# Turning normalised rows by a product with a diagonal of their roots in a hybrid trunk kernel on one core

## The chip, the cores and the metric

The kernel runs on one core of a Trainium2 chip. A core has five engines that run side by side: TensorE (PE; its weight loads are shown apart as PEld), VectorE (DVE), ScalarE (ACT), GpSimd (POOL) and SyncE (SP, which here only starts DMA transfers). They share a buffer memory of 128 partitions (SBUF); PE writes its results into eight accumulator banks (PSUM), from which DVE and ACT read them. The metric is the device time of one execution in microseconds. Lower is better.

## The reference

One layer over 2048 rows of 1024 channels, all in fp32. What matters for the change is that the rows are normalised three times and that two of these feed products which contract over the channels:

```python
def rmsnorm(x, g):
    y = xf * lax.rsqrt(jnp.mean(xf * xf, axis=-1, keepdims=True) + EPS) * g
...
xn = rmsnorm(x, norm1_g[l])
z = xn @ w_in[l]
u_pool, zq, zf, zi, zo, zg = jnp.split(z, splits, axis=-1)
gates = jax.nn.sigmoid(zg + b_gate[l]).reshape(B, S, N_BRANCHES, D_MODEL)
ya = pool_mixer(u_pool, pool_w[l], pool_scale[l]) @ w_pa[l]
yb = hgrn2_mixer(zq, zf, zi, zo, lower_bounds[l], hgrn_norm_g[l]) @ w_pb[l]
merged = gates[:, :, 0] * ya + gates[:, :, 1] * yb
x = x + merged @ w_o[l]
x = x + conv_glu_ffn(rmsnorm(x, norm2_g[l]), w_up[l], conv_w[l], conv_b[l], w_down[l])
return rmsnorm(x, final_g)
```

The root of a row is one number for each row; the gain `g` is one number for each channel.

## The kernel before

**Tiling.** The 2048 rows are four row blocks of 512 rows (`TB`), each of four row tiles of 128 rows (`NT`, index j). The 1024 channels are eight column blocks of 128 (index k). Two row blocks at a time go through the mixer (`mixer`, b0 = 0 and 2) and then through the feed-forward part (`ffn`). The large products are done by a Strassen scheme of seven products in place of eight (P1 to P7), each operand split into a high and a low part and multiplied in three products of 128x128 by 128x512, all through the helper `mm` (L157 and L158).

**Rows and channels.** The products need the operand with channels on the partitions, but the sum of squares is taken along a row. So a row tile is normalised with rows on the partitions and then turned in blocks of 128x128 on PE. This is done for the first two row blocks of x (called x0 and x1, at the start of the kernel) and for all four row blocks of the mixer's output (m0 and m1 after the first mixer, m2 and m3 after the second). The row blocks 2 and 3 of x come by another way: `channels_a_task` and `channels_b_task` load them with channels on the partitions already, and nothing is turned there.

**The steps for one row tile** (`norm_rows`, L772 to L784). Its two halves of 128x512 (`halves`, from the dictionary `xt`) are squared and summed on ScalarE by `row_rstd` (L762 to L770), which writes the squares into two tiles `t` that nobody reads; GpSimd makes the root's inverse `r`, one number for each row, in two small steps (L768, L769). VectorE then multiplies each half by `r` into the same two tiles `t` (L782), and these become `xs[j, 0]` and `xs[j, 1]`. Last comes `after(j)`: for m it stores the unscaled rows to DRAM for the later sum (`spill_rows`, L881 to L888), for x0 it turns the blocks that are wanted first.

**Turning** (`transpose`, L868 to L870). One call turns the block of row tile j and column block k into a quarter of an accumulator bank, with PE's transpose and the unit matrix `ident`. Four calls (j = 0 to 3) fill the bank of one column block. ScalarE or VectorE then reads the bank, multiplies by the channel gain and writes the operand or its two parts.

**Who calls it.** `forms_a_task` normalises and turns the first row block of a pair (x0, m0, m2) and makes the forms B11 and B21; `forms_b_task` does so for the second (x1, m1, m3) and makes the Strassen differences (T1 to T4, B22). At the very start (`early`) the column blocks 0 to 3 of x0 are turned row tile by row tile, as soon as each is normalised, and between them stand transposes of the unit matrix that only keep PE busy (`warm`, L747 to L752). Everywhere else the four blocks of a column block are turned together. In `forms_b_task` a condition (`go`) holds the turning back until a given place in the stream of products.

**The order.** Tasks are Python generators that are stepped once in every six products of the main stream, so the turning is issued between products. Each engine runs its instructions in the order in which the build put them, and that order is worked out from estimated times (`schedule_with_timeline_sim=True`, L2132). Working tiles come from a pool of 73 buffers of 128x528 (`slot`); a buffer is free when the last instruction that uses its tile is done.

Of the kernel before, what the change touches and what calls it, by code (L numbers as in the profile page):

```python
# [15 lines left out]
ALU = mybir.AluOpType  # L16
AX = mybir.AxisListType

P = 128
# [70 lines left out]
def tile_trunk(  # L90
# [17 lines left out]
    pe, act, dve, pool, sp = nc.tensor, nc.scalar, nc.vector, nc.gpsimd, nc.sync  # L108
# [10 lines left out]
    def slot(name, cols=TB, dt=F32):  # L119
        return slots.tile([P, cols], dt, tag="s", name=name, padded_shape=[P, 528])  # L120
# [249 lines left out]
    kept, keeping, w_both, halves = {}, [], {}, {}  # L370
# [259 lines left out]
    ident = const.tile([P, P], F32, tag="ident", name="ident")  # L630
# [131 lines left out]
    def row_rstd(halves, junk, name):  # L762
        ss = small.tile([P, 4], F32, tag="ssq", name=name + "ss")
        for hf in range(2):
            act.activation(junk[hf], halves[hf], AF.Square, scale=1.0 / 32.0,
                           accum_out=ss[:, hf : hf + 1])
        r = small.tile([P, 4], F32, tag="rstd", name=name + "r")
        pool.tensor_scalar(r[:, 1:2], ss[:, 1:2], ss[:, 0:1], EPS, ALU.add, ALU.add)  # L768
        last_root[0] = pool.tensor_tensor(r[:, :1], r[:, 1:2], neghalf[:, :1], ALU.pow)  # L769
        return r  # L770

    def norm_rows(src, name, xs, after, lag=1):  # L772
        for j in range(NT):
            while (src, j) not in ready:
                yield 1
            halves = [xt[src, j, c] for c in range(2)]
            t = [slot(f"{name}xs{j}_{hf}") for hf in range(2)]
            r = row_rstd(halves, t, f"{name}{j}")
            if lag:
                yield lag  # L780
            for hf in range(2):
                dve.tensor_scalar(t[hf], halves[hf], r[:, 0:1], None, ALU.mult)  # L782
                xs[j, hf] = t[hf]
            after(j)  # L784

    def load_channels(b, k):
# [80 lines left out]

    def transpose(ps, xs, j, k):  # L868
        c = (k % 4) * P
        return pe.transpose(ps[:, j * P : (j + 1) * P], xs[j, k // 4][:, c : c + P], ident)  # L870

    def transposed(xs, k, name, gain, ps=None):
        if ps is None:
            ps = bank(f"{name}t{k}")
            for j in range(NT):
                transpose(ps, xs, j, k)
        t = slot(f"{name}b{k}")
        act.activation(t, ps, AF.Copy, scale=col(gain + k))
        return t
# [10 lines left out]
    def forms_a_task(src, gain, forms, full, after=lambda j: None, early=False):  # L890
# [4 lines left out]
        def rows(j):  # L895
            after(j)
            for k in range(len(pts)):
                ins = transpose(pts[k], xs, j, k)
            if early:
                warm(WARM[1], ins)  # L900

        if early:
            warm(WARM[0])
        yield from norm_rows(src, name, xs, rows)
        yield 6

# [15 lines left out]
        for k in range(len(pts), KD):  # L922
            key = "B11" if k < 4 else "B21"
            if early:
                ps = bank(f"{name}t{k}")
                for j in range(NT):
                    transpose(ps, xs, j, k)
                scaled(k, key, ps)
                t = slot(f"{name}b{k}")
                dve.tensor_scalar(t, ps, col(gain + k), None, ALU.mult)  # L930
                full[key].append(t)
                yield 1
                continue
            t = transposed(xs, k, name, gain)
            yield 1
            full[key].append(t)
            forms[key].append(split(t, f"{name}f{k}", True))

    def forms_b_task(src, gain, forms, full, after, go, early):
        name = f"{src[0]}{src[1]}_"  # L940
        xs = {}
        while early and not forms["B21"]:
            yield 1
        yield from norm_rows(src, name, xs, after, int(early))
        while not go():
            yield 2
# [371 lines left out]
    class Unit:  # L1318
# [34 lines left out]
        def after(self, p):  # L1353
            bk, t = self.bank, self.t
            if p == "P1":
                act.copy(self.tmp("e1"), bk["X"])  # L1356
            elif p == "P6":
                first(dve.tensor_tensor(self.tmp("u2"), t["e1"], bk["Z"], ALU.subtract))
            elif p == "P2":
                self.emit(0, 0, None, bk["X"])  # L1360
            elif p == "P7":
                if self.own:
                    ins = dve.tensor_tensor(self.tmp("u3"), bk["W"], t["u2"], ALU.subtract)
                else:
                    ins = dve.tensor_tensor(self.tmp("u3"), bk["Z"], t["e1"], ALU.subtract)
                first(ins)
                self.forms.setdefault("u3", []).append(ins)
                self.emit(1, 1, (t["u3"], "add"), bk["V"])
            elif p == "P4":
                if self.own:  # L1370
                    self.emit(1, 0, (t["u3"], "add"), bk["Y"])
                else:
                    self.emit(1, 0, (t["e1"], "from"), bk["Z"])
            elif p == "P3":
                self.emit(0, 1, (t["u2"], "sub"), bk["V"])
# [760 lines left out]
```

## Time and profile before

| what | value |
|---|---|
| median of 3 runs | 2460.93 us (2460.14 to 2461.15) |
| the profiled execution | 2461.48 us |
| its span | 2459.8 us |
| instructions in the span | 37972 |
| mean clock granted to PE | 0.999 |
| HBM read / written | 403.55 MB / 200.81 MB |

The page of the profile gives busy times by engine, the chain of work that ended last and the costliest groups of instructions. More precise answers come from views of the same trace: one line's instructions, busy time by stage, the waits of one engine, and the chain in order of time. In the chain a row is a start and a length in us and what the chain went through there; "x4" is the number of instructions merged. In the view of one line, three durations (shortest, median, longest, in ns) stand behind the count. In the view by stage a row is a stretch of time and its length, then the busy time and number of instructions on PE, PEld, DVE, ACT and POOL, then the granted clock, the DMA share and GB/s. In the view of waits a row is who waited for whom, the total in us, how many times, and the longest. Matmuls are pipelined, so the duration of one is longer than the time that it adds to a busy PE.

### The profile page before, as it was taken

The numbers are of one execution on the slowest core, as the hardware profiler recorded it, in microseconds if no ns is written. First come the engines' busy times: TensorE is split into PE (matmuls) and PEld (weight loads), VectorE is DVE, ScalarE is ACT, GpSimd is POOL, SyncE is SP. The second block draws the span as 40 slices with busy tenths as digits, with TensorE's granted clock in tenths as the row PEclk, the third lists the DMA queues.
The fourth block names the chain that finished last, engine by engine and source line by source line (L and its number), as shares of the span: only waits on it lengthen the run. The fifth ranks groups of instructions, "written<-read, shape, count | busy, mean of one in ns | idle before, by whom it ended". The sixth has DMA issues, their size and how long they took to land.

```text
span 2459.8 us, 37972 instructions
## 1 busy us (share of the span) xinstructions
PE 2439.1 (99%) x12624; PEld 1979.3 (80%) x12624; DVE 1903.0 (77%) x3294; ACT 1232.0 (50%) x2372; POOL 750.7 (31%) x1068
## 2 busy tenths in 40 slices
PE   9999999999999999999999999999999999999998
PEld 7887777788888888888888888888888888888887
DVE  7777776997998778876586667768889987878755
ACT  6545544435555445555544555542465554445534
POOL 4343353403354334451210101112033332335310
PEclk9999999999999999999999999999999999999999
DMA  8989888977888779899784443478333444447852
GB/s 283 312 218 277 237 220 238 329 221 245 206 251 242 225 226 240 269 364 321 237 285 153 136 127 122 154 237 306 112 129 129 150 156 134 145 144 260 306 165 99
DMA packets 272612, 529.29 MB, mean 215 GB/s; under 512 B 28640, under 2 KB 49248, under 8 KB 272096
## 3 DMA queue, kind: packets, MB, share of 16 engines
q1 hardware_dynamic: 204560, 348.47, 42.4%
q0 software_dynamic: 42880, 113.27, 18.1%
q10 hardware_dynamic: 24976, 65.13, 7.6%
q8 instruction: 99, 1.62, 0.3%
q14 instruction: 97, 0.79, 0.1%
HBM read 403.55 MB, written 200.81 MB: 246 GB/s over the span
## 4 chain that ended last, share of the span: by engine, by line
PE 92%; DVE 3%; DMA 2%; ACT 1%; issue 1%; POOL 0%; SPq 0%; ACTq 0%; DVEq 0%; POOLq 0%
PE dn_P L158 17%; PE up_Z L158 15%; PE up_X L158 10%; PE up_V L158 10%; PE wo_P L158 6%; PE gr_V L158 3%; PE pb L158 3%; PE gr_X L158 3%; PE io_Z L158 2%; PE io_V L158 2%; PE gr_W L158 2%; PE gr_Y L158 2%; PE fr_X L158 1%; PE gr_Z L158 1%; PE fr_V L158 1%; PE ur_X L158 1%
## 5 line engine op out<-in xcount | busy, mean ns | idle before, releaser
L260 ACT CAST ops<-raw 128x512 fp32r<-128x512 f32 x802 | 493.4, 620 | 784.8 <-PE dn_P L158 161.5
L266 DVE TENSOR_TENSOR ops<-raw,ops 128x512 fp32r<-128x512 f32 x774 | 571.4, 743 | 240.9 <-ACT ops L260 232.6
L1872 DVE SCALAR_TENSOR_TENSOR e<-h,cols,e 128x512 f32<-128x512 f32 x176 | 142.9, 817 | 30.3 <-ACT e L1870 26.9
L1870 ACT ACTIVATE e<-h,cols 128x512 f32<-128x512 f32 x176 | 142.2, 814 | 25.3 <-DVE h L1316 18.9
L1875 DVE SCALAR_TENSOR_TENSOR e<-h,cols,e 128x512 f32<-128x512 f32 x176 | 133.9, 770 | 2.5
L1125 POOL DMA_DIRECT2D g_P<-dg_P x154 | 83.0, 541 | 171.8 <-PE dn_P L158 133.0
L1441 POOL TENSOR_TENSOR gf_P<-e,e 128x512 f32<-128x512 f32 x44 | 61.1, 1390 | 149.5 <-DVE e L1881 85.8
L1441 POOL TENSOR_TENSOR gf_P<-gf_P,e 128x512 f32<-128x512 f32 x44 | 58.2, 1322 | 74.1 <-DVE e L1881 71.6
L501 POOL TENSOR_TENSOR raw<-raw,raw 128x512 f32<-128x512 f32 x32 | 46.5, 1453 | 90.7 <-DVE ops L266 81.8
L1879 ACT ACTIVATE e<-e 128x512 f32<-128x512 f32 x88 | 55.6, 632 | 36.6 <-DVE e L1875 36.4
L1865 POOL COPY h<-h 128x2 f32<-128x2 f32 x88 | 39.3, 459 | 106.6 <-DVE h L1315 103.8
L1316 DVE TENSOR_TENSOR h<-up_u,up_V 128x512 f32<-128x512 f32 x88 | 60.1, 683 | 10.5 <-PE up_V L158 10.0
L1867 POOL COPY hist<-h 128x2 f32<-128x2 f32 x88 | 35.2, 400 | 101.5 <-DVE h L1316 99.3
L1413 DVE TENSOR_TENSOR x<-x,wo_P 128x512 f32<-128x512 f32 x88 | 55.8, 678 | 11.8 <-PE wo_P L158 11.7
L1865 POOL COPY h<-hist 128x2 f32<-128x2 f32 x88 | 45.0, 517 | 55.4 <-DVE h L1316 25.1
L1581 POOL TENSOR_TENSOR q<-q,qs 128x512 f32<-128x512 f32 x16 | 22.3, 1393 | 119.2 <-ACT qs L1580 119.2
L1413 DVE TENSOR_TENSOR ac<-ac,dn_P 128x512 f32<-128x512 f32 x72 | 47.3, 681 | 11.5 <-PE dn_P L158 11.0
L1614 ACT ACTIVATE gt<-gt,cols 128x512 f32<-128x512 f32 x48 | 34.8, 724 | 42.5 <-DVE gt L1316 41.3
L1356 ACT COPY up_e<-up_X 128x512 f32<-128x512 f32 x44 | 25.8, 587 | 60.1 <-PE up_X L158 38.6
L1895 POOL DMA_DIRECT2D dg_P<-gf_P x88 | 50.7, 576 | 8.9 <-POOL gf_P L1441 7.2
L758 POOL TENSOR_SCALAR ro<-so 128x4 f32<-128x4 f32 x16 | 4.1, 256 | 151.3 <-ACT sq L1289 151.1
L1755 POOL TENSOR_TENSOR ya<-ya,gl 128x512 f32<-128x512 f32 x24 | 35.8, 1512 | 47.2 <-DVE ya L1752 39.6
(1335 smaller groups left out, 7855.2 us busy)
## 6 DMA issues: line engine op xcount, KB each, us to landing
g_P<-dg_P POOLq DMA_DIRECT2D x154, 256.0 KB, 5.9
raw<-in_w_up_t SPq DMA_DIRECT2D x132, 256.0 KB, 3.1
raw<-in_w_in_t SPq DMA_DIRECT2D x98, 256.0 KB, 3.7
dg_P<-gf_P POOLq DMA_DIRECT2D x88, 256.0 KB, 3.8
dg_P<-e SPq DMA_DIRECT2D x66, 256.0 KB, 3.2
raw<-in_w_dn SPq DMA_DIRECT2D x66, 256.0 KB, 5.4
x<-in_x SPq DMA_DIRECT2D x64, 256.0 KB, 5.2
gd<-gt ACTq DMA_DIRECT2D x64, 256.0 KB, 3.6
```

Source lines behind the costliest of these rows:

```text
L158: count[1] = pe.matmul(*args, **kw)
L260: self.mark = act.copy(hi, v)
L266: low = self.low = dve.tensor_tensor(lo, v, f32(hi), ALU.subtract)
L1125: eng.dma_start(t, d)
L1316: return dve.tensor_tensor(dst, t, ps, ALU.add if how == "add" else ALU.subtract)
L1413: dve.tensor_tensor(t, t, ps[j], ALU.add if sg > 0 else ALU.subtract)
L1441: pin(eng.tensor_tensor(t, x0, x1, op))
L1865: pool.tensor_copy(h[:, 0:2], hist[:, mt] if hf == 0 else hs[s, 0][:, TB : TB + 2])
L1870: in_turn(act.activation(t, h[:, 2:], AF.Identity, bias=col(o_cb + mt), scale=col(o_cw + 4 * MF + mt)))
L1872: in_turn(second(dve.scalar_tensor_tensor(t, h[:, 1 : 1 + TB], col(o_cw + 2 * MF + mt), t, ALU.mult, ALU.add)))
L1875: dve.scalar_tensor_tensor(t, h[:, 0:TB], col(o_cw + mt), t, ALU.mult, ALU.add)
L1879: in_turn(act.activation(g, g, AF.Silu))
```

## The change

VectorE no longer scales the rows. For each row tile it multiplies the 128x128 unit matrix by the row tile's inverse root, which gives a diagonal matrix; the four diagonals of a row block stand side by side in one new working tile (`roots`). The blocks of the unscaled halves are turned by an ordinary fp32 product with that diagonal instead of a transpose with the unit matrix. The product of a block's transpose with the diagonal scales each row by its root, so that the bank holds what it held before. The tiles `t` now hold only the squares.

```diff
@@ -774,13 +774,16 @@
             while (src, j) not in ready:
                 yield 1
             halves = [xt[src, j, c] for c in range(2)]
+            if not j:
+                roots = slot(f"{name}dg")
             t = [slot(f"{name}xs{j}_{hf}") for hf in range(2)]
             r = row_rstd(halves, t, f"{name}{j}")
             if lag:
                 yield lag
             for hf in range(2):
-                dve.tensor_scalar(t[hf], halves[hf], r[:, 0:1], None, ALU.mult)
-                xs[j, hf] = t[hf]
+                xs[j, hf] = halves[hf]
+            xs[j] = roots[:, j * P : (j + 1) * P]
+            dve.tensor_scalar(xs[j], ident, r[:, 0:1], None, ALU.mult)
             after(j)
 
     def load_channels(b, k):
@@ -867,7 +870,8 @@
 
     def transpose(ps, xs, j, k):
         c = (k % 4) * P
-        return pe.transpose(ps[:, j * P : (j + 1) * P], xs[j, k // 4][:, c : c + P], ident)
+        return pe.matmul(ps[:, j * P : (j + 1) * P], xs[j, k // 4][:, c : c + P], xs[j],
+                         start=True, stop=True)
 
     def transposed(xs, k, name, gain, ps=None):
         if ps is None:
```

## The prediction

> **What bounds the kernel now.** I read the head of the page first, then its chain of work that ended last.
>
> ```profile
> span 2459.8 us, 37972 instructions
> ...
> PE 2439.1 (99%) x12624; PEld 1979.3 (80%) x12624; DVE 1903.0 (77%) x3294; ACT 1232.0 (50%) x2372; POOL 750.7 (31%) x1068
> ...
> PE 92%; DVE 3%; DMA 2%; ACT 1%; issue 1%; POOL 0%; SPq 0%; ACTq 0%; DVEq 0%; POOLq 0%
> ```
>
> PE is busy for 99% of the span and makes up 92% of the chain; DVE, which the change relieves, is 77% busy and makes up 3%. So the first question is not what DVE saves but what each instruction costs on PE. Busy time over the whole span says little about one place, so the next view is busy time by stage. I cut it where blocks are turned: the head (x0 and x1, up to 60 us), the two stretches in which the m rows are turned (583 to 619 and 1790 to 1826 us), and what lies between.
>
> ```profile
> 0.00:14.00 14.00, 9.16 (x61) 8.07 (x61) 5.64 (x16) 8.72 (x22) 6.33 (x19) 1.00 0.87 303
> 14.00:60.00 46.00, 45.00 (x219) 36.82 (x219) 39.05 (x63) 28.73 (x58) 24.03 (x64) 1.00 0.84 275
> 60.00:300.00 240.00, 238.82 (x1745) 192.28 (x1744) 180.73 (x422) 127.46 (x289) 88.67 (x84) 1.00 0.89 262
> 300.00:583.00 283.00, 277.36 (x1469) 223.67 (x1468) 231.01 (x406) 122.23 (x260) 91.09 (x84) 1.00 0.82 251
> 583.00:619.00 36.00, 36.00 (x191) 29.75 (x190) 28.00 (x44) 22.52 (x46) 16.53 (x20) 1.00 0.76 225
> 619.00:1790.00 1171.00, 1170.35 (x6062) 952.07 (x6061) 900.59 (x1558) 584.88 (x1121) 313.95 (x462) 1.00 0.71 222
> 1790.00:1826.00 36.00, 36.00 (x191) 29.80 (x190) 27.98 (x44) 22.74 (x47) 14.21 (x19) 1.00 0.41 136
> ```
>
> The first number after the stage's length is PE's busy time. Both stretches in which m is turned have PE at 36.00 of 36.00 us, so nothing there waits for the scaling that is removed, and any time added to PE there lengthens the run. In the head PE is idle for 14.00 - 9.16 = 4.84 us before 14 us and for 46.00 - 45.00 = 1.00 us from 14 to 60 us. The granted clock is 1.00 everywhere.
>
> **The change part by part.** First, how many blocks are turned, and by how many records. The answer for the transposes' line (L870), and for two lines of the recurrence that serve as a yardstick (L1252 transposes, L1261 an ordinary fp32 product), has these rows.
>
> ```profile
> L870 PE MATMUL m_t<-ident,m_xs x128: 269/272/274, 583.6 to 1824.9; 128*128 128x128 f32 x128
> L870 PE MATMUL x_t<-ident,x_xs x64: 269/273/329, 7.5 to 41.4; 128*128 128x128 f32 x64
> ```
> ```profile
> L1252 PE MATMUL pk<-ident,k x60: 270/273/273, 154.7 to 1606.8; 128*128 128x128 f32 x60
> ```
> ```profile
> L1261 PE MATMUL pv<-v,kt x120: 270/275/276, 161.2 to 1621.2; 128*128 128x128 f32 x120
> ```
>
> Six row blocks (x0, x1, m0 to m3) of 4 row tiles and 8 column blocks make 192 turned blocks, and there are 128 + 64 = 192 records: a transpose is one record. L1252 and L1261 run over the same loop (nk chunks, 4 heads, 4 row blocks, 15 chunks a head in all: 60 calls), but the product leaves 120 records: an ordinary fp32 product of 128x128 by 128x128 is **two records**. The changed line is a product of just this form: fp32 on both sides, 128x128 by 128x128, start and stop set.
>
> Second, what each takes on a busy PE. The durations above (about 0.27 us) overlap and are not it; the chain in order of time gives what each group adds.
>
> ```profile
> 154.88 0.87 PE pk L1252 x8
> ...
> 161.34 0.89 PE pv L1261 x8
> ...
> 168.84 0.22 PE po L1284 x2
> ```
> ```profile
> 585.58 0.44 PE m_t L870 x4
> ...
> 608.15 0.87 PE m_t L870 x8
> ```
>
> A turned block of m takes 0.44 / 4 = 0.11 us of PE. A product takes 0.89 / 4 = 0.2225 us (eight records are four products), and the po row says the same: 0.22 for one. All of these lie inside the same kind of stream of 128x512 products. So each block turned costs **0.2225 - 0.11 = 0.1125 us more on PE**. I take this price for all 192; the rows of product and transpose scatter by less than 0.005 us, so its bounds are 0.11 and 0.115.
>
> The m rows: 128 blocks x 0.1125 = **14.4 us**, all of it in stages where PE has no idle time. Nothing hides it.
>
> The x rows in the head: 64 blocks. The first 16 (columns 0 to 3 of x0) stand in the start, row tile by row tile, each waiting for its scaling; there only the last row tile counts, because PE idles between them.
>
> ```profile
> 12.31 0.50 DVE x_xs L782
> 12.81 0.04 issue
> 12.85 0.66 PE x_t L870 x4
> 13.51 0.55 PE warm L750 x5
> 14.06 5.74 PE io_X L158 x24
> ```
>
> Today the first scaling of 0.50 us lets the four transposes go. The change puts one 128x128 scaling of the unit matrix there. No row shows that operation; the nearest are these, the same operation on 512 columns and on 4.
>
> ```profile
> L782 DVE TENSOR_SCALAR x_xs<-x,x_0r x4: 479/482/488, 7.0 to 25.2; 128x512 f32<-128x512 f32 x4
> ```
> ```profile
> 5.32 0.17 DVE L2077 TENSOR_SCALAR lbt<-lbt 128x4 f32<-128x4 f32 x1
> ```
>
> Between 0.17 and 0.48 us in proportion to the columns I estimate 0.17 + 0.31 x 124 / 508 = 0.25 us. PE then starts the last group at 12.31 + 0.25 + 0.04 = 12.60 us and not at 12.85, but needs 4 x 0.1125 = 0.45 us more before the warming transposes and io_X: **+0.2 us** at the start (+0.1 with 0.17 us, +0.4 with 0.48 us).
>
> The other 48 blocks (columns 4 to 7 of x0, all of x1) follow up to 42 us (the L870 row above) and cost 48 x 0.1125 = **5.4 us**. Against that stands the 1.00 us of idle time from 14 to 60 us. The waits of PE show what it is.
>
> ```profile
> PE io_Z L158 <- ACT ops L260: 0.5, 1, 0.5
> PE io_V L158 <- ACT ops L260: 0.5, 1, 0.5
> ```
>
> Both are waits for a converted weight, and the chain before them leads back through DVE and a DMA, not through PE:
>
> ```profile
> 29.10 0.79 DVE x_xs L782 x2
> ...
> 31.21 0.67 DVE x_xs L782
> 31.88 0.64 DVE w8s L432
> 32.52 0.65 DVE w9s L432
> ...
> 34.97 5.01 DMA kw1ioP<-w9s
> ```
>
> Here is the one place where DVE's relief matters. The eight scalings of x1 are part of the chain that makes the sums w8s and w9s late. They become four of an estimated 0.25 us, so that chain gets shorter by at most 8 x 0.48 - 4 x 0.25 = 2.8 us, while PE comes later by up to 5.4 us. PE then finds its weights ready: I take the whole **1.0 us** off. Were that cover not there (the chain moves with PE), nothing comes off.
>
> What else moves. On DVE 48 scalings of 0.48 us or more go and 24 of about 0.25 us come, some 17 us of DVE busy time in all; in the m stretches PE is at 36.00 of 36.00, so that is worth nothing there. ScalarE's squares and GpSimd's two steps for the root stay as they are. No DMA is added or moved on any queue, the spill of the m rows included. The added wait, of a turning product for its piece of the diagonal, takes the place of the wait for two scaled tiles and ends earlier by one scaling; behind it on PE stands the whole stream, as before. The x and m tiles stay in use until the last product has read them and the tiles of the squares are free at once: eight buffers held change places with eight, and one more of 73 is held for the diagonal. I cost that at nothing; its cover is that PE waits for no buffer in the stretches at 36.00 of 36.00.
>
> **Sum:** 14.4 + 5.4 + 0.2 - 1.0 = 19.0 us. The profiled execution took 2461.48 us, of which 2459.8 are the span; 2461.48 + 19.0 = 2480.5. The median of the runs shown is 2460.93 us, 0.55 us below the profiled one, so I say **2480 us**, 0.8% slower.
>
> One rule of the Trainium skill gives another sum. By the rows, a product is two records of 0.11 us against one for a transpose. The page "TensorE: Matmul & The Clock Gate", section "Terms", calls the transpose mode four times faster for fp32, and "FP8 and Floating Point Precision", section "TensorE Precision Notes", counts four passes for a true fp32 product. By that rule each block would cost three further transposes; the rows of pv and po disagree with it, as they show twice and not four times.
>
> **The rivals.**
> 1. *Four times the transpose.* If the product with the diagonal runs as four passes of 0.11 us, each block costs 0.33 us more: 192 x 0.33 = 63 us, less 1 us, about 2524 us. For it: nothing here shows a product with a diagonal. Against it: pv has the same shapes and types and takes 0.2225 us. Chance 0.03.
> 2. *The second record is hidden: no change.* PEld is 80% busy and PE may set the two records of a product between the long ones at no further cost, as a block has the same data to load. Then the extra cost is nothing, the start gains 0.25 us and the head 1.0 us: about 2460 us. It decides below (4.9 + 1.2) / 192 = 0.032 us of extra cost for a block, where the result is within 0.2%. Against it: the pv group stands in just such a stream and shows no hiding at all. Chance 0.04.
> 3. *Another order.* The build orders each engine's instructions by estimated times, and other instructions give other estimates. PE's idle time outside the head and the tail is 1.18 + 5.64 + 0.65 = 7.5 us (the stages from 60 to 583 us and from 619 to 1790 us, less their busy time). A new order could bring that much again (2488 us) or give it back (2473 us). The largest waits of PE outside the head are these:
>
> ```profile
> PE pl L1155 <- ACT k L1138: 2.3, 3, 1.2
> ...
> PE pa_V L158 <- DVE ya L1752: 1.3, 3, 0.6
> ```
>
>    For it: they are waits of tenths of a microsecond that any shift moves. Against it: none is for a line that the change touches. Chance 0.15, with 0.10 of it on the slow side.
>
> **How the numbers follow.** The forecast has the remaining 0.78; its own range, from the prices' bounds with 0 to 2 us of absorbed idle time, is 2477 to 2484 us. The range of 8 in 10 takes in the third rival on both sides: **2473 to 2488 us**; the first two, 0.07 together, lie outside. About 0.2% (4.9 us) is what a measurement of this kernel can tell from no change. Forecast, first and third rival are slower by more: 0.95 with a small part of the third left out (0.78 + 0.03 + 0.14). The second gives "same" nearly all its 0.04. Faster is left 0.01: the extra cost would have to vanish and more waits than the two above with it.
>
> **What would show each step.** The line of the turning product should have 384 records, two for each block, and its groups should stand in the chain with 0.89 us for four blocks (1.78 for eight) where the transposes have 0.44 (0.87). The stages in which m is turned should each be about 7.2 us longer for the same products, and still full. DVE should show 24 scalings of 128x128 near 0.25 us in place of 48, and a sum lower by about 17 us. The two waits of io_Z and io_V for converted weights should be gone, and the io_X products should enter the chain near 14.3 us, not at 14.06. If the groups take 0.44 us, the second rival holds; if they take 1.76 us, the first. If the m stages are longer by 7.2 us but the sum is off by more than 3 us, the order elsewhere has changed, and the stages from 60 to 583 us will show it. What would make the prediction wrong is above all a price of the product that depends on what stands around it, since 192 of them carry the sum.

## The result and the profile after

| what | before | after |
|---|---|---|
| median of 6 runs each, us | 2461.04 (2460.14 to 2462.88) | 2479.43 (2478.01 to 2480.09) |
| ratio after / before, 95% interval | | 1.0073 (1.006 to 1.0086) |
| profiled execution, us | 2461.48 | 2480.01 |
| its span, us | 2459.8 | 2478.3 |

The change makes the kernel 18.4 us slower; 2480 us was predicted. The head of the page of after gives the span, the busy times and the shares of the chain:

```profile
span 2478.3 us, 38316 instructions
...
PE 2460.0 (99%) x12816; PEld 2001.9 (81%) x12816; DVE 1890.4 (76%) x3270; ACT 1232.9 (50%) x2372; POOL 740.2 (30%) x1068
...
PE 94%; DMA 2%; DVE 2%; ACT 1%; issue 1%; POOL 0%; SPq 0%; ACTq 0%; POOLq 0%; DVEq 0%
```

VectorE does 12.6 us less (1903.0 - 1890.4) and TensorE 20.9 us more, with 192 records more. The span follows TensorE. The view by stage of after, cut where blocks are turned, has the same columns as before:

```profile
0.00:14.00 14.00, 10.87 (x77) 10.02 (x77) 3.46 (x12) 8.95 (x22) 5.08 (x19) 1.00 0.85 295
14.00:60.00 46.00, 46.00 (x251) 39.45 (x250) 35.83 (x57) 28.00 (x58) 21.46 (x64) 1.00 0.86 277
60.00:300.00 240.00, 239.12 (x1746) 192.41 (x1745) 179.29 (x422) 127.30 (x289) 88.07 (x83) 1.00 0.88 257
300.00:583.00 283.00, 276.78 (x1469) 223.46 (x1468) 227.96 (x400) 121.49 (x260) 91.77 (x84) 1.00 0.82 250
583.00:627.00 44.00, 44.00 (x257) 38.33 (x256) 27.78 (x44) 22.96 (x48) 13.66 (x20) 1.00 0.70 216
627.00:1794.00 1167.00, 1166.32 (x6039) 947.23 (x6038) 893.72 (x1544) 580.95 (x1110) 308.97 (x458) 1.00 0.71 221
1794.00:1842.00 48.00, 48.00 (x276) 41.62 (x275) 31.10 (x49) 27.05 (x57) 14.06 (x23) 1.00 0.39 131
```

Three things are to be seen. The stages in which m is turned (583 to 627 and 1794 to 1842 us) are still full. The 1.00 us of idle time from 14 to 60 us is gone. And from 60 to 1794 us, outside those stages, PE is idle for 0.88 + 6.22 + 0.68 = 7.8 us, where it was 7.5 us: no new wait of any size has come. The instructions of the turning line and of the new scaling in after, with shortest, median and longest duration in ns:

```profile
L873 PE MATMUL m_t<-m_dg,x x256: 270/275/276, 587.4 to 1841.9; 128*128 128x128 f32 x128
L873 PE MATMUL x_t<-x_dg,x x128: 270/275/378, 7.3 to 42.9; 128*128 128x128 f32 x128
```
```profile
L786 DVE TENSOR_SCALAR m_dg<-ident,m_0r x4: 280/282/286, 572.9 to 1816.3; 128x128 f32<-128x128 f32 x4
L786 DVE TENSOR_SCALAR x_dg<-ident,x_0r x2: 285/290/294, 7.0 to 24.6; 128x128 f32<-128x128 f32 x2
```

There are 256 + 128 = 384 records where 192 stood. The chain of after in order of time, where m0 and then m1 are turned:

```profile
587.61 0.89 PE m_t L873 x8
588.50 1.40 PE wo_P L158 x6
...
615.65 1.78 PE m_t L873 x16
617.43 1.39 PE up_X L158 x6
```

Four blocks take 0.89 us and eight take 1.78 us, as the pv rows before, and six products of the main stream follow each group without a gap. How late the same product starts in the two kernels shows where the time comes in. The timeline of PE before, and then that of after, at the first product behind the mixer's weights (fr_X) and the first of the feed-forward part (up_X):

```profile
98.64 0.39 PE L158 MATMUL fr_X<-x_f0h,ops 128*128 128x512 f32 x1
...
598.72 0.39 PE L158 MATMUL up_X<-m_f0h,ops 128*128 128x512 f32 x1
```
```profile
102.46 0.39 PE L158 MATMUL fr_X<-x_f0h,ops 128*128 128x512 f32 x1
...
606.21 0.40 PE L158 MATMUL up_X<-m_f0h,ops 128*128 128x512 f32 x1
```

The head costs 102.46 - 98.64 = 3.8 us. By up_X, behind which m1 is still to be turned, it is 606.21 - 598.72 = 7.5 us. The same subtraction at nine products, for every kernel that ran, is the table on which most of what follows rests. Each number is the start of a product in that kernel's profile less its start in the profile of before, in us; the first row has the starts before. Between wo and up lies the turning of m0 (m2 in the second pair), behind up that of m1 (m3).

```
                       io_X   io_Z   fr_X     wo     up   io_X     wo     up   last
                      first  first  first  first  first  2nd pr 2nd pr 2nd pr product
before, start         13.96  42.22  98.65 517.10 598.72 1243.84 1723.87 1805.49 2452.04
after                 -0.02   4.74   3.81   3.84   7.49  12.00  12.23  15.93  18.51
before, again          0.25   0.25  -0.44   0.77   0.75   0.72   0.73   0.74   0.72
after, again          -0.46   4.30   3.38   1.40   5.05   9.55   9.79  13.48  16.07
scaled, product       -0.07   4.74   3.91   1.80   5.44   9.44   9.26  12.68  14.82
unscaled, transpose   -1.53  -2.27  -2.71  -2.89  -2.91  -2.74  -2.71  -2.68  -4.09
m only                -0.08  -0.07  -0.53  -0.65   2.93   7.43   7.61  11.12  14.16
x only                -0.52   4.28   3.36   1.41   1.49   2.83   2.26   2.27  -0.07
x only, again         -0.15   4.61   3.69   1.66   1.70   3.03   2.41   2.42   0.06
product twice          2.68  18.21  17.40  15.00  25.64  36.09  36.71  47.54  57.02
two halves             2.41  17.91  17.04  14.29  25.02  36.36  36.46  47.38  57.32
one record             4.92   4.65   3.86   4.33   4.30   9.95  10.32  10.37  11.37
```

In the row of after, m0 and m2 cost 7.49 - 3.84 = 3.65 and 15.93 - 12.23 = 3.70 us, where 32 x 0.1125 = 3.6 us were predicted. From up to the next mixer it is 4.51 us and from the second up to the last product 2.58 us: m1 and m3 lie in there, with something added to one and taken from the other, to which the runs below come back.

### The profile page after: what moved, and what is told of

Read it like the earlier page. It is cut to its first block, busy times and chain, and to the rows that moved or that the text cites. A ratio compares the mean times of both kernels' runs of the same rounds, so it can differ in the third digit from the quotient of the medians.

```text
span 2478.3 us, 38316 instructions
## 1 busy us (share of the span) xinstructions
PE 2460.0 (99%) x12816; PEld 2001.9 (81%) x12816; DVE 1890.4 (76%) x3270; ACT 1232.9 (50%) x2372; POOL 740.2 (30%) x1068
## 4 chain that ended last, share of the span: by engine, by line
PE 94%; DMA 2%; DVE 2%; ACT 1%; issue 1%; POOL 0%; SPq 0%; ACTq 0%; POOLq 0%; DVEq 0%
PE dn_P L158 17%; PE up_Z L158 15%; PE up_V L158 10%; PE up_X L158 10%; PE wo_P L158 6%; PE gr_V L158 3%; PE pb L158 3%; PE gr_X L158 3%; PE io_Z L158 3%; PE io_V L158 2%; PE gr_W L158 2%; PE fr_X L158 1%; PE gr_Z L158 1%; PE gr_Y L158 1%; PE fr_V L158 1%; PE m_t L873 1%
```

## The experiments

The expectations name theories by letters. **A** is the prediction's: TensorE pays for a second record in each block, and nothing else counts. **B** is the first rival to it, that the product costs more than that and VectorE's relief pays some of it back. **C** is that part of the cost comes from another order of the work behind the head. **D** is that the second record's price depends on what stands around it, so that part of it is hidden. **E** and **F** came up on the way: a pace of the main stream that belongs to the program, and a wait that differs between executions. A time is a median, a ratio stands with its 95% interval, and the kernel before ran beside each on the same chip.

**1. The product without the relief of VectorE.** The rows are scaled as before and turned by an ordinary product with the unit matrix.

```diff
-        return pe.transpose(ps[:, j * P : (j + 1) * P], xs[j, k // 4][:, c : c + P], ident)
+        return pe.matmul(ps[:, j * P : (j + 1) * P], xs[j, k // 4][:, c : c + P], ident,
+                         start=True, stop=True)
```

> VectorE scales the rows as before, and PE turns them by an fp32 product with the unit matrix: the change's PE part alone. Theory A (the time is 192 blocks at 0.1125 us more on PE, and VectorE's relief is worth next to nothing): 2461.0 + 14.4 (m) + 5.4 (x behind the start) + 0.45 (start) less 1 to 1.5 us of idle time in the head = about 2479.5 us, within 1 us of the changed kernel. Theory B (the product costs more than that, and VectorE's 13 us of saved busy time pay part of it back): 3 us or more above the changed kernel, 2482.5 us or more.

Measured: 2477.29 us beside 2461.66 us, +15.6 us, ratio 1.0063 (1.0051 to 1.0076). The chain of this kernel at m0:

```profile
585.55 0.89 PE m_t L870 x8
586.44 1.40 PE wo_P L158 x6
```

The group has the price of after with VectorE's work as before, and the whole cost is not above that of after (+18.4 us, and +16.2 us when it ran again). B would need it above. So B falls: the record accounts for all of it, and no relief is seen. In the head the row is that of after to within 0.1 us (4.74 and 3.91), though VectorE still scales: TensorE's lateness alone covers the two waits for converted weights.

**2. The relief without the product.** The diagonals are made, but the unscaled rows are turned by the transpose with the unit matrix, so that these rows are not normalised.

```diff
-        return pe.matmul(ps[:, j * P : (j + 1) * P], xs[j, k // 4][:, c : c + P], xs[j],
-                         start=True, stop=True)
+        return pe.transpose(ps[:, j * P : (j + 1) * P], xs[j, k // 4][:, c : c + P], ident)
```

> The diagonals are made as in the change, but the unscaled rows are turned by the transpose with the unit matrix: VectorE's part of the change alone. The normalisation of these rows is left out. Theory A: 2460 to 2461 us, at most 1 us below the kernel before, since only the head has a wait behind the scaling. Theory B: 2458 us or less.

Measured: 2457.75 us beside 2461.66 us, -3.9 us, ratio 0.9987 (0.9978 to 0.9996). That is more than A allows (1 us), and it lies in the range given for B (2458 us or less). The chain of this kernel at the start:

```profile
11.79 0.59 ACT x_f0h L912
12.39 0.04 issue
12.43 5.81 PE io_X L158 x24
```

No transpose waits for a root any more, so io_X starts at 12.43 and not at 13.96 us (-1.5 us). Another 1.2 us goes by fr_X (-2.71 in all), where the two waits for weights stood; the m stages give nothing (-2.89 at wo, -2.68 at the second up); the last 1.4 us goes in the second feed-forward part, where it is the pace of the products (232.48 and 231.70 ns in the table under runs 8 to 10, 1840 x 0.78 ns = 1.4 us). So to be rid of the waits for VectorE's scalings is worth some 2.7 us in the head, and nothing in the stages where m is turned. It pays nothing back in after, as run 1 shows.

**3 and 4. The change for one kind of row alone.** For m only, and for x only; the other kind is scaled and transposed as before.

```diff
+            if not j and src[0] == "m":        # "x" in the other kernel
+                roots = slot(f"{name}dg")
...
+                if src[0] == "m":
+                    xs[j, hf] = halves[hf]
+                    continue
...
+        if j not in xs:
+            return pe.transpose(to, rows, ident)
+        return pe.matmul(to, rows, xs[j], start=True, stop=True)
```

> The change for the m rows alone (128 blocks); x as before. Theory A: 2461.0 + 128 x 0.1125 = 2475.4 us, the m stages each 7.2 us longer. Theory C (part of the 18.4 us comes from another order of the work behind the head): less than 12 us or more than 17 us above the kernel before.

> The change for the x rows alone (64 blocks); m as before. Theory A: 48 x 0.1125 = 5.4 us less the two waits of the head, which cost 1.5 us of the stream, and nothing at the start: 2461.0 + 3.9 = 2465 us. If the idle time of 1.0 us is all that goes: 2465.5 us. Theory C: under 2463 or over 2467 us, and not the rest that m only leaves of 18.4 us.

Measured: m only 2476.36 us, +14.7 us, ratio 1.006 (1.0048 to 1.0073); x only 2461.87 us, +0.2 us, ratio 1.0001 (0.9992 to 1.001), both beside 2461.66 us. The m rows cost what the prediction's term says (14.4 us). The x rows should have cost 4.6 us by the prediction and 3.9 us by the expectation above. In the head they come near it: the table has 4.28 us at io_Z and 3.36 us at fr_X. Then it is lost again: 2.0 us by wo, and 2.3 us between the second up and the last product, hundreds of microseconds behind the last x block. A step that costs 3 us where it stands was worth nothing at the end. The time lies in the range given for C (under 2463 us), and the two parts make 14.9 us and not 18.4, as C has it. A, which holds for m only, misses x only by 3 us: what happens behind the head counts too. Runs 8 to 10 ask what it is.

**5. Twice the cost.** Every turning product of after is issued twice.

```diff
+        for _ in range(2):
+            ins = pe.matmul(ps[:, j * P : (j + 1) * P], xs[j, k // 4][:, c : c + P], xs[j],
+                            start=True, stop=True)
+        return ins
```

> The changed kernel with every turning product issued twice into the same place. Theory A (a product is 0.2225 us of a full PE, nothing of it hidden): 176 blocks behind the start x 0.2225 = 39.2 us, and 2.4 us at the start, where the first groups already follow one another: 2479.4 + 41.6 = 2521 us. Theory D (PE has room between the long products, which the second record only partly fills): 2510 us or less.

Measured: 2518.58 us beside 2460.82 us, ratio 1.0233 (1.0218 to 1.0248), 39.2 us over after, where A gave 41.6. The chain of this kernel at m0:

```profile
598.64 1.78 PE m_t L874 x16
600.42 1.39 PE wo_P L158 x6
```

Four blocks take 1.78 us, twice 0.89 to the hundredth. The price doesn't depend on how much of it stands there, and nothing is hidden: D falls. 192 x 0.2225 = 42.7 us would be the plain sum. By the table, against after, the parts with turning give 13.6 us (fr_X), 7.0 (m0), 7.1 (m2) and 6.9 (m3), each near its due (14.2 with the start's 16 blocks, and 7.1 for each m); the stretch from fr_X to wo, without any turning, gives 2.4 us back, and the stretch with m1 1.2 us less than its due. The latter is the pace of the products there (231.39 ns for 232.07 in the table under runs 8 to 10, 1.2 us over the up products).

**6. The same columns in twice the records.** Each product is cut in two, of 64 columns of the diagonal each.

```diff
+        for h in range(0, P, 64):
+            ins = pe.matmul(ps[:, j * P + h : j * P + h + 64], xs[j, k // 4][:, c : c + P],
+                            xs[j][:, h : h + 64], start=True, stop=True)
+        return ins
```

> The changed kernel with every turning product cut into two of 64 columns of the diagonal each: the same columns go through PE, but each block is loaded as a weight four times instead of twice. If the columns streamed set the 0.11 us of a record: 2479.4 us as the changed kernel, four records of 0.055 us. If the weight load sets it: four records of about 0.1 us or more, 2513 us or more.

Measured: 2520.32 us beside 2460.82 us, ratio 1.0247 (1.023 to 1.0265); the four executions lie between 2518.82 and 2528.75 us. The chain of this kernel at m0, and its turning line:

```profile
597.98 1.73 PE m_t L874 x16
599.71 1.46 PE wo_P L158 x6
```
```profile
L874 PE MATMUL m_t<-m_dg,x x512: 217/275/275, 597.8 to 1880.4; 128*128 128x64 f32 x171
```

Sixteen records of 64 columns take 1.73 us, 0.108 us each, where eight of 128 columns take 0.89 us, 0.111 us each. Half the columns cost the same. What a record of this shape costs is thus not its moving columns. Nor does every record cost this much. In the chain of before, 64 records with a stationary block of 32 columns and 48 moving columns take 0.013 us each:

```profile
203.96 0.82 PE pl L1155 x64
```

What is left is the stationary block of 128x128, which is the same in both kernels. That it sets the price is argued, as no run changed it alone. The Trainium skill, page "TensorE: Matmul & The Clock Gate", section "LDWEIGHTS (loading the stationary operand)", gives a load as the stationary operand's columns divided by 1.2, in ns: 128 / 1.2 = 107 ns by estimate, and this trace agrees with 0.108 us for this shape. For 32 columns it would give 27 ns by estimate, where the pl records, which write to separate quarters of the partitions in turn, add 13 ns each: the agreement is for this shape alone.

**7. One record.** VectorE scales the rows into new tiles of type fp32r, and these are turned by an fp32r product with a unit matrix of that type; the rows lose their last bits.

```diff
+                xs["unit"] = slot(f"{name}un", P, F32R)
+                dve.tensor_scalar(xs["unit"], ident, 1.0, None, ALU.mult)
...
+                xs[j, hf] = slot(f"{name}xr{j}_{hf}", dt=F32R)
+                dve.tensor_scalar(xs[j, hf], halves[hf], r[:, 0:1], None, ALU.mult)
...
+        return pe.matmul(ps[:, j * P : (j + 1) * P], xs[j, k // 4][:, c : c + P], xs["unit"],
+                         start=True, stop=True)
```

> VectorE scales the rows as before, but writes them as fp32r, and PE turns them by an fp32r product with a unit matrix in fp32r; the rows lose their last bits. An fp32r product of the main stream is one record. Theory A (the cost is the second record): 2461 us, within 1.5 us of the kernel before, the groups of four blocks at 0.44 us in the chain. If a product costs more than a transpose whatever its records: above 2466 us.

Measured: 2470.05 us beside 2460.82 us, +9.2 us, ratio 1.0036 (1.0023 to 1.0048). The chain of this kernel at m0, and the longest wait of its PE:

```profile
589.88 0.40 PE m_t L873 x4
590.27 2.83 PE wo_P L158 x12
```
```profile
PE x_t L873 <- DVE x_xr L786: 6.5, 3, 3.2
```

With one record a block takes 0.40 / 4 = 0.10 us, and m0 adds nothing (4.33 at wo, 4.30 at up). So an ordinary product isn't dear in itself: its second record is, which here goes away together with the fp32 type. The time that A gave (2461 us) failed all the same, and lies in the range of the theory against it (above 2466 us), which the row of the group refutes. It failed because the start is 4.9 us later (TensorE waits 6.5 us for scaled tiles there) and the stretch with m1 takes 5.7 us more. In that stretch the view by stage shows PE no longer full (PE busy 56.96 of 60.00 us):

```profile
600.00:660.00 60.00, 56.96 (x252) 45.08 (x251) 48.25 (x73) 34.89 (x67) 22.43 (x29) 0.97 0.82 194
```

Why these tiles come so late wasn't tried; only the price of the record and m0 are clean in this run.

**8 to 10. The same programs again.** Before, after and x only ran once more, unedited, each with a new profile.

> The kernel before once more, with its own profile. Theory E (the program's order fixes the waits of the mixer's last stage and the pitch of the main stream): the same wait of about 0.6 us for gr_V, the same 232.5 ns from product to product in the second feed-forward part and 231.7 in the first, as in the profile shown; ratio 1. Theory F (each execution has its own): the wait moves by 1 us or more or the pitch by 0.5 ns or more.

> The changed kernel once more, on one chip with the two others. 2479.4 us by the first measurement, 18.4 us over the kernel before. Theory E: again 2.2 us of waiting for gr_V and 232.07 ns in both feed-forward parts. Theory F: another wait, another pitch, and a time that still differs from 18.4 us by less than 1.5 us, as the turning itself (18.3 us in the profile) does not change.

> The change for the x rows alone once more: 2461.9 us at first, 0.2 us over the kernel before, where its head is 3.2 us longer. Theory E: again within 0.5 us of 2461.9, with a shorter wait for gr_V (0.2 us) and 231.4 ns in the second feed-forward part. Theory F: the head is again 3 to 4 us longer, and the rest comes out otherwise, so that the time lies up to 3.9 us over the kernel before.

Measured, beside 2461.66 us: before 2461.11 us, ratio 0.9999 (0.9989 to 1.0009); after 2477.87 us, ratio 1.0067 (1.0052 to 1.0082); x only 2461.65 us, ratio 1.0002 (0.9993 to 1.0011). All three agree with their first runs within the intervals. What differs between two profiles of one program is one wait, the first row of PE's waits of after and its row in after, again:

```profile
PE gr_V L158 <- DVE gt L1320: 2.2, 1, 2.2
```
```profile
PE gr_V L158 <- DVE gt L1320: 0.4, 1, 0.4
```

The same wait in before, and then in before, again:

```profile
PE gr_V L158 <- DVE gt L1316: 0.6, 1, 0.6
```
```profile
PE gr_V L158 <- DVE gt L1316: 1.8, 1, 1.8
```

In the table the first row of after goes from 3.81 at fr_X to 3.84 at wo, and the second from 3.38 to 1.40: 2.0 us between the two executions, and the wait's 1.8 us is nearly all of it. The chain of after leads back from this wait to a DMA that loads tiles of the mixer again:

```profile
418.58 5.26 DMA mx<-md
...
430.43 0.61 DVE gr_u L1367
431.04 0.02 issue
431.07 0.70 DVE gt L1320
431.76 0.14 issue
431.90 3.01 PE gr_V L158 x12
```

That is F, and for before and after it holds: the same program waits 1 to 2 us longer in one execution than in another. It doesn't hold everywhere. In x only the wait was 0.2 us both times, and after, again lies 2.2 us below its first cost, where F gave 1.5 us at most. A rival stands beside it, that a late head shortens these waits by itself. Between fr_X and wo, six of the eight profiles with a late head lose 2.0 to 2.8 us, and none of the other three does (-0.2 to +1.2 us); the two exceptions are after and one record. The runs don't take the two apart.

E concerns the rest. The mean time from the start of one product to the next in the two feed-forward parts, from the starts in the trace, in ns. The up products are 1840 pairs in each part (so that 1 ns makes 1.84 us; 1842 pairs where the m rows are turned by products), and the dn products behind them 922:

```
                   up first  dn first  up second  dn second
before               231.73    231.47     232.48     231.76
before, again        231.72    231.47     232.47     231.76
after                232.07    231.58     232.07     231.26
after, again         232.07    231.58     232.07     231.26
x only               232.28    231.82     231.43     231.33
x only, again        232.28    231.81     231.42     231.33
m only               232.04    231.63     232.33     231.25
scaled, product      231.81    231.50     231.45     232.01
unscaled, transp.    231.73    231.64     231.70     231.78
product twice        231.39    231.60     231.77     231.59
```

Each program that ran twice repeats its own pace to 0.01 ns, and programs differ by up to 1 ns. For x only it is -1.05 ns in the second part, 1840 x 1.05 = 1.9 us, and the dn products take another 922 x 0.43 = 0.4 us: together the 2.3 us that went there. In the first part the same count gives 1.0 + 0.3 us, the 1.3 us that came. It also settles the two stretches of after that were left open. Counted from the first start of each group of turning records to the start of the product behind it, m1 and m3 take 3.8 us more each (6.81 for 3.00 us); the pace adds 0.7 us in the first part and takes 1.2 us in the second, which makes the 4.51 and 2.58 us of the table to within 0.03 us. So E holds for the pace, though not for the wait of gr_V in before and after: that x only costs nothing in the sum is a coincidence of a head that costs 3.4 us, a wait and a pace. What sets the pace is open. Another allotment of tiles to buffers, which changes when tiles live longer, might do it, but the records hold no addresses, and it wasn't tried.

## Why the prediction was right

**The price of a block.** It said 0.2225 - 0.11 = 0.1125 us, from a yardstick of the same shapes and types (pv against pk). The groups came out at 0.89 and 1.78 us, run 5 doubled them, and run 7 took the second record away and the cost with it. Run 6 adds that a record of this shape isn't paid by its moving columns.

**The m rows.** 14.4 us predicted; 3.65 (m0) and 3.70 us (m2) at the landmarks, and 14.7 us for m only as a whole. By the count of groups each stage of m is 7.5 us longer (13.27 for 5.75 us), where 7.2 was foreseen. That is 0.1175 us a block, a little over the upper bound of 0.115. The argument that nothing hides it, because those stages are full, held.

**The x rows, the start and the two waits.** 5.4 + 0.2 - 1.0 = 4.6 us predicted, 3.8 us measured at fr_X. Two terms were mis-sized. The start: the chain of after shows it.

```profile
12.14 0.29 DVE x_dg L786
12.43 0.04 issue
12.47 1.16 PE x_t L873 x8
13.63 0.55 PE warm L750 x5
14.18 5.50 PE io_X L158 x24
```

io_X enters the chain at 14.18 us (14.3 predicted, 14.06 before), and its first product starts within 0.02 us of before. The diagonal was a little dearer than estimated (0.29 for 0.25 us), but its root was ready earlier, as the last section shows. The other profiles of the same programs scatter by some 0.4 us here, so this term was below what can be told. The two waits: 5.4 - 3.83 = 1.6 us came off between io_X and fr_X, where 1.0 us of idle time had been counted. A product is recorded as lasting 0.39 us, while the next one starts after 0.23 us; idle time counted from the recorded end misses the difference, 0.16 us for each wait, which is a part of the 0.6. The waits went as foreseen, but VectorE's shorter chain wasn't needed for it (run 1).

**VectorE's relief.** Costed at nothing in the m stages, and rightly (run 2). Its size was mis-sized: 12.6 us less busy time (14.0 in the second pair of profiles), and not 17. The scalings themselves did fall by 17.7 us, from 25.2 to 7.5 us by the sum of their recorded durations; other instructions of VectorE took longer in after.

**Nothing elsewhere.** This is the step that doesn't hold as it was put. In after, 3.8 us of head and four row blocks at 3.6 us make 18.2 of the 18.5 us, but only because the rest cancels: gr_V waits 1.6 us longer while other waits before wo become shorter, the m rows are 0.6 us dearer than 14.4, and the pace adds 0.7 us in the first feed-forward part and takes 1.2 us in the second. The third rival had foreseen shifts of this size by another order of instructions; they came as one wait at the end of a DMA and as the pace. Its range (2473 to 2488 us) was wide enough for them. The sum came out within 1 us, which is luck, as it is closer than its parts deserve: the same program gave +18.4 and +16.2 us in two measurements. The forecast's own range, 2477 to 2484 us, is also wider than the bounds named for it: 176 x 0.11 + 0.1 - 2.0 = 17.5 us and 176 x 0.115 + 0.4 = 20.6 us give 2478 to 2482 us.

**The rivals.** Four passes fell with the first group (0.89, not 1.76 us). The hidden second record fell with the same row, and with run 5.

No kernel that ran beats before and does the same work: the largest gain, 3.9 us, is that of run 2, which leaves out the normalisation of these rows.

## What to carry to other kernels

Moving work from an engine that is 77% busy to one that is 99% busy was priced here by the second alone: count the records that it adds there, find the same shape and type in the same kind of stream, and multiply. An fp32 product by a diagonal is two records where a transpose is one, and cutting the columns that it streams saves nothing (a record costs 0.108 us with 64 and 0.111 us with 128). And a change of some 2 us that stands in the head can be undone or doubled far behind it, so two parts of a change need not add up: compare the starts of the same product along the whole run before explaining a total.

## What was not expected of the hardware

**The pace of a stream belongs to the program.** The same up products run at means from 231.4 to 232.5 ns in different programs, and the three that ran twice repeat to 0.01 ns in another execution. Over the 1840 products of one feed-forward part a difference of 1 ns is 1.8 us, about half of the head's whole cost.

**GpSimd's small steps slow down beside VectorE's scalings.** The two steps for the last root of x0, in the timeline of POOL before, and then of after:

```profile
10.43 0.87 POOL L768 TENSOR_SCALAR x_3r<-x_3ss 128x1 f32<-128x1 f32 x1
11.38 0.90 POOL L769 TENSOR_TENSOR x_3r<-x_3r,neghalf 128x1 f32<-128x1 f32 x1
```
```profile
10.60 0.30 POOL L768 TENSOR_SCALAR x_3r<-x_3ss 128x1 f32<-128x1 f32 x1 [0.35 <-ACT x_xs L765]
10.98 0.56 POOL L769 TENSOR_TENSOR x_3r<-x_3r,neghalf 128x1 f32<-128x1 f32 x1
```

Beside them VectorE before ran the two scalings of the row tile ahead (x_2r), of 512 columns each, and a sum of two weights:

```profile
10.37 0.89 DVE L782 TENSOR_SCALAR x_xs<-x,x_2r 128x512 f32<-128x512 f32 x2 [0.76 <-POOL x_2r L769]
11.18 0.68 DVE L266 TENSOR_TENSOR ops<-raw,ops 128x512 fp32r<-128x512 f32 x1
```

The step that takes 0.30 us alone lasted 0.87 us, until the scalings were done. In after the diagonal that stands in their place was over before the step began (10.28 to 10.57 us), and the root was ready 12.28 - 11.54 = 0.7 us earlier; most of this was lost again because the diagonal stood behind a sum of weights in VectorE's order. The Trainium skill, page "SBUF — State Buffer", section "Who interferes with whom", states that VectorE and GpSimd share a pair of ports, which an instruction of the kind of tensor_scalar can hold to its end while the other engine is blocked. The two timelines agree with it, with 0.87 against 0.30 us; no run here took the cause apart.
